# A streaming encoder step: three engines' queues in written order, units of 2048, softmax in ten pieces

## The chip, the cores and the metric

The kernel runs on one core of one Trainium2 chip. The metric is the device time of one execution in microseconds; the time before is 1638.82 us, the median of three runs (1638.69, 1638.82, 1639.95).

## The reference, cut to what matters

One layer of an encoder, for a prompt of 256 frames and a sample of 64 frames, which share the weights; D_MODEL is 2048, there are 8 heads of 128, 8 gating groups of 128, and 5632 is the width of the FFN. All is float32.

```
xn = rmsnorm(x)
q, k, v, u, vs, g = split(xn @ w_in)           # 5 x 1024 columns and 2 x 2048 gates
z = q k^T / sqrt(128); mask = k_pos < q_pos    # stick-breaking attention
log_stay = where(mask, log_sigmoid(-z), 0)
log_rest = cumsum(log_stay, reverse) - log_stay
a = where(mask, exp(log_sigmoid(z) + log_rest), 0) @ v
u, vs = gelu(u), rmsnorm(gelu(vs))
bb = u * (masked w_spatial @ vs + b_spatial)
g_a, g_b = sigmoid(g + b_gate)
merged = g_a * (a @ w_branch_a) + g_b * (bb @ w_branch_b)
h = x + merged @ w_out
h = h + (silu(hn @ w_gate) * (hn @ w_up)) @ w_down     # hn = rmsnorm(h)
y = rmsnorm(h)
```

New k, v and vs rows are outputs too. The sample's attention also sees 256 cached rows of k and v.

## The kernel before, in words

All 320 frames are the columns of every product; the 2048 features lie in 16 blocks of 128 partitions. Weights come from memory as blocks of 128 x 128, eight in a DMA of 512 KB issued on SP's queue, and each block is used once. A value is split into a high and a low part, and a product takes three matmuls for a weight block: high by high, high by low, low by high (`product`, L92 to L97). Two forms of the split are used:

- *Plain* (`weights`, `block`, L81 to L111): ACT casts the weights to fp32r (L87), DVE subtracts (L88). It serves the first six head blocks (`WHOLE`), all of `w_out`, and the first three pairs of the FFN (`PLAIN`).
- *Scaled fp16* (`Group`, L276): four tiles of 1024 columns share one scale. DVE takes a tile's largest value (L173) or ACT the sum of its absolutes (L178), DVE packs them (`pack`, L184, L186), one matmul spreads them over the partitions (`spread`, L190, into a bank of the products' own pool), DVE makes a power of two (`close`, L194). Then ACT writes the high half (L325) and DVE the low half (L326) right ahead of the matmuls that use them. It serves all the rest.

Features get their norm by `Features.normed` (L271): DVE multiplies by the factor of the column (L273), then `half` (L136) takes ACT's high half (L138) and DVE's low half (L139). A norm's root is taken on POOL (L219), copied on ACT (L224) and transposed on DVE (L226).

A *step* is eight weight blocks, thus 24 matmuls; `tick()` ends it, and `at(step, fn)` puts off work to the end of a step. I count steps from the end of the start stage, which makes q, k and v of heads 0 and 1 as x and the weights come in. Steps 0 to 11 are the six plain head blocks; 12 to 43 the other heads, with the spatial gate's `vs` and `us` behind them; then gates and the products by `w_a` and `w_b`; the plain products by `w_out` (32 steps); then the FFN, whose first 12 steps are plain. The attention goes by pairs of heads (`attend`, L713): `att_scores` (L587) takes the scores and the whole softmax (Abs, Exp and Ln on ACT at L617 to L619, scans on DVE, Exp), `att_turn` transposes the weights in 16-bit planes by a DMA on SP's queue, `att_join` (L546) puts them together on DVE, `att_out` (L664) multiplies by v, all between the steps of the heads that follow. One preload (L613) brings a table that holds both Exp and Ln.

The start stage is ordered by hand. Behind it a scheduler orders each engine's queue, but for instructions marked `keep_in_program_order`; SBUF holds ten raw tiles of 1024 and six split ones.

Of the kernel before, what the change touches and what calls it, by code (L numbers as in the profile page):

```python
# [33 lines left out]
AHEAD = 3  # L34
WHOLE = 6
BACK = 4
SLOTS = 49
RAW = 10
SPLIT = 6
LAG = 2  # L40
# [6 lines left out]
def stream_step(ctx: ExitStack, tc: tile.TileContext, xT, w_in, w_a, w_b, w_out, w_gu, w_down,  # L47
# [16 lines left out]
    def aux1():  # L64
        return psum.tile([P, 512], F32, tag="aux1", bufs=1, name="aux1")
# [5 lines left out]
    def at(tick, fn, *a):  # L71
        assert tick > state["tick"], (tick, state["tick"])
        later.setdefault(tick, []).append((fn, a))

    def tick():
        state["tick"] += 1
        for fn, a in later.pop(state["tick"], ()):
            fn(*a)


    def weights(src, n, view=lambda t: t):  # L81
        raw = wraw.tile([P, HALF * P], F32, tag="raw", bufs=RAW, name="raw")
        d = nc.sync.dma_start(out=view(raw[:, : n * P]), in_=src)
        if state["tick"] < 4:
            tc.keep_in_program_order(d)
        wh, wl = (wsplit.tile([P, HALF * P], F32R, tag="w", bufs=SPLIT, name=t) for t in ("wh", "wl"))
        nc.scalar.copy(out=wh[:, : n * P], in_=raw[:, : n * P])  # L87
        nc.vector.tensor_tensor(out=wl[:, : n * P], in0=raw[:, : n * P],  # L88
                                in1=wh[:, : n * P].bitcast(F32), op=ALU.subtract)
        return wh, wl  # L90
# [8 lines left out]
    def block(src, act, on=None):  # L99

        ps = acc()
        nk = len(act)
        if on is not None:
            nc.scalar.copy(out=ps[:, :T], in_=on)
        for k0 in range(0, nk, HALF):
            n = min(HALF, nk - k0)
            w = weights(src[:, k0 * P : (k0 + n) * P], n)
            for j in range(n):
                product(ps, w, j, act[k0 + j], on is None and k0 + j == 0, k0 + j == nk - 1)
            tick()  # L110
        return ps[:, :T]  # L111
# [54 lines left out]
    class Scale:  # L166

        def __init__(self, n, room):
            self.n, self.room = n, room
            self.tops = const.tile([P, n], F32, tag=f"tops{n}", bufs=2, name="tops")  # L170

        def top(self, i, src):
            tc.keep_in_program_order(nc.vector.tensor_reduce(  # L173
                out=self.tops[:, i : i + 1], in_=src, axis=mybir.AxisListType.X, op=ALU.max, apply_absolute_value=True))

        def sum(self, i, src, junk):
            tc.keep_in_program_order(
                nc.scalar.activation(out=junk, in_=src, func=AF.Abs, accum_out=self.tops[:, i : i + 1]))  # L178
# [9 lines left out]
        def spread(self):  # L188
            self.row = acc()
            tc.keep_in_program_order(nc.tensor.matmul(self.row[:, :P], self.own.to_broadcast([P, P]), turner, start=True, stop=True))  # L190
# [63 lines left out]
    class Features:  # L254
# [16 lines left out]
        def normed(self, m, src, factor):  # L271
            t = t320("ev")
            nc.vector.tensor_tensor(out=t, in0=src, in1=got[factor], op=ALU.mult)  # L273
            self.half.append(half(t, self.gain[:, m : m + 1]))

    class Group:  # L276

        def __init__(self, tiles, start, undo, by_vector, lead=(9, 7), first=0, home=None, late_undo=False):
            self.tiles, self.undo_of, self.by_vector, self.raw, self.home = tiles, undo, by_vector, [], home or wraw_tile
            n, now = len(tiles), state["tick"]  # L280
            for i in range(n):
                begin = max(start - lead[0] + i, first + i, now + 1)
                check = max(start - lead[1] + i, begin + 2)
                at(begin, self.load, i)
                at(check, self.top, i)
            ready = max(start + n - lead[1], check + 1)
            assert ready < start, (start, ready)
            at(ready, lambda: self.scale.spread())
            at(ready + 1, lambda: self.scale.close())
            at(max(ready + 1, start if late_undo else 0), self.settle)  # L290

        def load(self, i):
            src, n = self.tiles[i]
            raw = self.home()
            nc.sync.dma_start(out=raw[:, 0 : n * P], in_=src)
            self.raw.append(raw[:, 0 : n * P])

        def top(self, i):
            if i == 0:
                self.scale = Scale(len(self.tiles), W_ROOM)  # L300
            if i in self.by_vector:
                self.scale.top(i, self.raw[i])
            else:
                self.scale.sum(i, self.raw[i], junk[:, 0 : self.raw[i].shape[1]])
            if i == len(self.tiles) - 1:
                self.scale.pack()
# [9 lines left out]
        def block(self, i, n, x, on=None):  # L316
            ps, k = acc(), 0
            if on is not None:
                nc.scalar.activation(out=ps[:, :T], in_=on[0], func=AF.Copy, scale=on[1])
            nk = sum(c for _, c in self.tiles[i : i + n])  # L320
            for raw in self.raw[i : i + n]:
                w, up = raw.shape[1], self.scale.up
                both = wsplit.tile([P, 2, HALF * P], F16, tag="w", bufs=SPLIT, name="w16")
                wh, wl = both[:, 0], both[:, 1]
                nc.scalar.activation(out=wh[:, :w], in_=raw, func=AF.Copy, scale=up)  # L325
                nc.vector.scalar_tensor_tensor(out=wl[:, :w], in0=raw, scalar=up, in1=wh[:, :w],  # L326
                                               op0=ALU.mult, op1=ALU.subtract)
                for j in range(w // P):
                    product(ps, (wh, wl), j, x[k], on is None and k == 0, k == nk - 1)
                    k += 1  # L330
                tick()
            return ps[:, :T]

    class Acts:
# [4 lines left out]
        def add(self, r):  # L339
            self.scale.top(len(self.raw), r)  # L340
            self.raw.append(r)
            if len(self.raw) == self.n:
                now = state["tick"]
                at(now + 1, self.scale.pack)
                at(now + 2, self.scale.spread)
                at(now + 3, self.close)
                for k in range(self.n):
                    at(now + 3 + k // 3, self.split, k)
# [11 lines left out]
    def wraw_tile():  # L360
        return wraw.tile([P, HALF * P], F32, tag="raw", bufs=RAW, name="raw16")

    def tiles_of(w, k0=0, n=KD):
        return [(w[:, (k0 + k) * P : (k0 + min(k + HALF, n)) * P], min(HALF, n - k)) for k in range(0, n, HALF)]

    junk = const.tile([P, HALF * P], BF16, name="junk")
# [21 lines left out]
    def load_w(b, c, n):  # L388
        raw = wraw.tile([P, HALF * P], F32, tag="raw", bufs=RAW, name="raw0")
# [4 lines left out]
    def split_w(raw, n, chunks=None):  # L394

        if chunks and chunks.start:
            w = ws[-1]
        else:
            state["start"] = state.get("start", 0) + 1
            w = tuple(spool.tile([P, HALF * P], F32R, tag=t, name=t) if state["start"] % 4 == 0 else  # L400
                      wsplit.tile([P, HALF * P], F32R, tag="w", bufs=SPLIT, name=t) for t in ("wh", "wl"))
# [84 lines left out]

    attn = {}
    att_ctx = ExitStack()
    apool = att_ctx.enter_context(tc.tile_pool(name="attn", bufs=1))
    rooms = {}  # L490

    def gate_load():
        nc.gpsimd.memset(wso, 0.0)
        tc.keep_in_program_order(nc.sync.dma_start(out=wst.rearrange("p g t -> p (g t)"), in_=ws_t))
# [43 lines left out]
    def turn(src):  # L538
        to = planes("turned", src.shape[2])
        flat = lambda t: t.rearrange("p w n -> p (w n)")  # L540
        tc.keep_in_program_order(nc.sync.dma_start(
# [13 lines left out]
    def att_rows(p):  # L555
        cvt = attn[p]["cv"] = rooms["late"].tile([P, 2, 2, P], F32, tag="cv", name="cv")
        tc.keep_in_program_order(nc.sync.dma_start(out=cvt.rearrange("p i h d -> p i (h d)"),
# [29 lines left out]
    def att_scores(p):  # L587
        s = attn[p]
        q, k, qp = s["q"], s["k"], s["qp"]
        za, zs = (aux(), aux()), (aux(), aux())  # L590
# [4 lines left out]
        for j in range(2):  # L595
            for b in range(2):
                nc.tensor.matmul(zs[j][:, 0 : KT - TP], s["qs"][:, j].rearrange("p w t -> p (w t)"), s["ks"][j][b],
                                 start=b == 0, stop=b == 1)
        z = s["z"] = pair("z0"), pair("z1")[:, 0 : Z + TS]
# [491 lines left out]
```

## Time and profile before

| | |
|---|---|
| median of 3 runs | 1638.82 us |
| profiled execution, device time | 1640.53 us |
| its span | 1638.7 us |
| mean granted clock of the matmul engine | 0.991 |
| PE busy | 1600.8 us, 98% |
| DVE busy | 1135.5 us, 69% |
| ACT busy | 1012.3 us, 62% |
| POOL busy | 59.2 us, 4% |
| read from memory | 256.03 MB, 160 GB/s over the span |

The numbers are of one profiled execution, and the span is the time from its first to its last instruction. PE is the matmul engine, PEld its weight loads, DVE the vector engine, ACT the scalar engine, POOL the general one, SP the queue that issues most DMAs. Busy shares are means over stages with different limits; what a change in a stage is worth is read in that stage.

### The profile page before, as it was taken

The numbers are of one execution on the slowest core, as the hardware profiler recorded it, in microseconds if no ns is written. First come the engines' busy times: TensorE is split into PE (matmuls) and PEld (weight loads), VectorE is DVE, ScalarE is ACT, GpSimd is POOL, SyncE is SP. The second block draws the span as 40 slices with busy tenths as digits, with TensorE's granted clock in tenths as the row PEclk, the third lists the DMA queues.
The fourth block names the chain that finished last, engine by engine and source line by source line (L and its number), as shares of the span: only waits on it lengthen the run. The fifth ranks groups of instructions, "written<-read, shape, count | busy, mean of one in ns | idle before, by whom it ended". The sixth has DMA issues, their size and how long they took to land.

```text
span 1638.7 us, 28858 instructions
## 1 busy us (share of the span) xinstructions
PE 1600.8 (98%) x11662; PEld 1224.7 (75%) x11662; DVE 1135.5 (69%) x2013; ACT 1012.3 (62%) x1503; POOL 59.2 (4%) x80
## 2 busy tenths in 40 slices
PE   9979989999999999999999999999999999999997
PEld 9966657777777777999877777777777777777775
DVE  6978778986666674557866667666666776666785
ACT  6676776776566663445866666456666755665662
POOL 0111002000000000111000000000000000000000
PEclk9989989999999999999999999999999999999998
DMA  9557654654544554557554555445555454444421
GB/s 326 174 146 215 166 154 141 191 177 159 165 154 155 156 173 150 176 174 253 182 165 164 163 167 165 154 155 156 164 166 161 139 192 155 155 151 140 124 64 65
DMA packets 100518, 268.40 MB, mean 164 GB/s; under 512 B 28992, under 2 KB 35392, under 8 KB 100384
## 3 DMA queue, kind: packets, MB, share of 16 engines
q1 hardware_dynamic: 97936, 261.36, 50.7%
q0 software_dynamic: 1312, 3.80, 0.7%
q8 instruction: 91, 1.49, 0.4%
q10 hardware_dynamic: 1136, 1.39, 0.2%
q14 instruction: 43, 0.35, 0.1%
HBM read 256.03 MB, written 5.51 MB: 160 GB/s over the span
## 4 chain that ended last, share of the span: by engine, by line
PE 86%; DVE 6%; ACT 3%; DMA 3%; issue 1%; POOL 0%; SPq 0%; DVEq 0%; ACTq 0%; POOLq 0%
PE acc L97 28%; PE acc L95 28%; PE acc L96 28%; PE aux L415 1%; DMA raw<-w_in 1%; DMA turned<-wp 1%; PE acc L415 1%; DVE half L139 1%; DVE w L326 1%; DVE e L627 1%; DVE wl L88 1%; DVE tops L173 1%; DVE ev L273 0%; ACT wp L536 0%; DMA raw<-w_gu 0%
## 5 line engine op out<-in xcount | busy, mean ns | idle before, releaser
L97 PE MATMUL acc<-half,w 128*128 128x320 f16 x3232 | 968.4, 300 | 6.7 <-DVE w L326 6.6
L95 PE MATMUL acc<-half,w 128*128 128x320 f16 x3232 | 968.3, 300 | 1.1 <-DVE q L690 0.5
L96 PE MATMUL acc<-half,w 128*128 128x320 f16 x3232 | 968.2, 300 | 0.0
L326 DVE SCALAR_TENSOR_TENSOR w<-raw,up,w 128x1024 f16<-128x1024 f32 (+1 forms) x412 | 517.8, 1262 | 142.6 <-ACT w L325 133.2
L325 ACT ACTIVATE w<-raw,up 128x1024 f16<-128x1024 f32 (+1 forms) x412 | 454.6, 1122 | 198.7 <-DVE up L196 179.9
L97 PEld LDWEIGHTS <-w 128*128 128x128 f16 x3232 | 316.4, 98 | 140.7 <-DVE w L326 9.1
L95 PEld LDWEIGHTS <-w 128*128 128x128 f16 x3232 | 316.5, 98 | 123.8 <-ACT w L325 0.7
L96 PEld LDWEIGHTS <-w 128*128 128x128 f16 x3232 | 316.4, 98 | 120.2 <-issue 1.2
L178 ACT ACTIVATE junk<-raw 128x1024 bf16<-128x1024 f32 x263 | 274.7, 1044 | 33.1 <-DMA raw<-w_b 19.3
L173 DVE TENSOR_REDUCE tops<-raw 128x1 f32<-128x1024 f32 (+1 forms) x149 | 171.9, 1154 | 12.2 <-DMA raw<-w_in 12.2
L194 DVE TENSOR_REDUCE peak<-acc 128x1 f32<-128x128 f32 x118 | 33.8, 286 | 166.1 <-PE acc L190 165.9
L941 ACT ACTIVATE bb<-acc,undo 128x320 f32<-128x320 f32 x41 | 21.6, 527 | 148.2 <-PE acc L97 144.3
L87 ACT CAST wh<-raw 128x1024 fp32r<-128x1024 f32 x56 | 58.6, 1046 | 73.2 <-PE acc L96 61.9
L88 DVE TENSOR_TENSOR wl<-raw,wh 128x1024 fp32r<-128x1024 f32 x56 | 68.4, 1222 | 31.5 <-ACT wh L87 27.8
L95 PE MATMUL acc<-mh,wh 128*128 128x320 f32 x256 | 79.3, 310 | 0.0
L96 PE MATMUL acc<-ml,wh 128*128 128x320 f32 x256 | 79.2, 309 | 0.0
L97 PE MATMUL acc<-mh,wl 128*128 128x320 f32 x256 | 79.2, 309 | 0.0
L965 DVE SCALAR_TENSOR_TENSOR h<-acc,undo,h 128x320 f32<-128x320 f32 x47 | 25.8, 548 | 57.0 <-PE acc L97 53.5
L178 ACT ACTIVATION_READ_ACCUMULATOR junk<-raw 128x1 f32 x263 | 49.3, 187 | 0.0
L95 PEld LDWEIGHTS acc<-mh,wh 128*128 128x128 f32 x256 | 48.1, 188 | 0.0
L96 PEld LDWEIGHTS acc<-ml,wh 128*128 128x128 f32 x256 | 48.1, 188 | 0.0
L97 PEld LDWEIGHTS acc<-mh,wl 128*128 128x128 f32 x256 | 48.1, 188 | 0.0
(224 smaller groups left out, 1205.5 us busy)
## 6 DMA issues: line engine op xcount, KB each, us to landing
raw<-w_gu SPq DMA_DIRECT2D x176, 512.0 KB, 4.5
raw<-w_in SPq DMA_DIRECT2D x141, 512.0 KB, 4.6
raw<-w_down SPq DMA_DIRECT2D x80, 512.0 KB, 4.2
raw<-w_out SPq DMA_DIRECT2D x32, 512.0 KB, 3.7
raw<-w_a SPq DMA_DIRECT2D x16, 512.0 KB, 3.6
raw<-w_b SPq DMA_DIRECT2D x16, 512.0 KB, 4.1
raw<-w_down SPq DMA_DIRECT2D x16, 256.0 KB, 3.4
x<-xT SPq DMA_DIRECT2D x8, 320.0 KB, 7.7
```

Of the source, the lines that this page charges most:

```text
L87: nc.scalar.copy(out=wh[:, : n * P], in_=raw[:, : n * P])
L88: nc.vector.tensor_tensor(out=wl[:, : n * P], in0=raw[:, : n * P], in1=wh[:, : n * P].bitcast(F32), op=ALU.subtract)
L95: nc.tensor.matmul(ps[:, :T], a, x[0], start=first, stop=False, skip_group_check=True)
L96: nc.tensor.matmul(ps[:, :T], a, x[1], start=False, stop=False, skip_group_check=True)
L97: nc.tensor.matmul(ps[:, :T], b, x[0], start=False, stop=last, skip_group_check=True)
L173: tc.keep_in_program_order(nc.vector.tensor_reduce(out=self.tops[:, i : i + 1], in_=src, axis=mybir.AxisListType.X, op=ALU.max, apply_abso ...
L178: nc.scalar.activation(out=junk, in_=src, func=AF.Abs, accum_out=self.tops[:, i : i + 1]))
L194: nc.vector.tensor_reduce(out=top, in_=self.row[:, :P], axis=mybir.AxisListType.X, op=ALU.max)
L325: nc.scalar.activation(out=wh[:, :w], in_=raw, func=AF.Copy, scale=up)
L326: nc.vector.scalar_tensor_tensor(out=wl[:, :w], in0=raw, scalar=up, in1=wh[:, :w], op0=ALU.mult, op1=ALU.subtract)
L415: nc.tensor.matmul(first[b][h][:, :T], w[:, (h * n + j) * P : (h * n + j + 1) * P], xs[c + j][i], start=not last and c + j + i == 0, stop= ...
L965: nc.vector.scalar_tensor_tensor(out=hs[i], in0=ps, scalar=g.undo, in1=hs[i], op0=ALU.mult, op1=ALU.add)
```

## The change

- Behind the start stage the queues of SP, ACT, DVE and PE are in the order in which the code issues (`manual_schedule`); only POOL's is left to the scheduler. Work that is due at the end of a step is sorted by a rank.
- `Plain` replaces `weights` and `block`: the load is issued eight steps ahead, the high half two steps ahead, the low half one.
- `Group` now has one unit of 2048 columns for each two steps (two units in the FFN), with a scale for each group: loads 10 (FFN: 14) steps ahead, bound 3 later, high half three steps ahead, low half two. There are 148 spreads instead of 118, and they have a bank of their own (`aux1`). SBUF holds five raw and three split units of 2048.
- Epilogues of products come one step later.
- `normed` multiplies in place (the x of the first norm) or into one buffer (`mg`, the FFN's).
- The softmax of a pair is in ten pieces from step +3 to +11 of the pair; its outputs come at +18. Pairs 0 to 3 begin at steps 10, 21, 33 and 45. The preload of the table of Exp and Ln is gone; the built program has 24 table loads (6 before).
- Four gate blocks are between the plain heads and the others (`EARLY_GATES`), evicted by a Copy, with their Sigmoid later; the gates lead the merge by 5 blocks (2 before).
- At the end the last block's residual is put into PSUM some steps ahead.

```diff
-    def at(tick, fn, *a):
+    def at(tick, fn, *a, rank=5):
+        if tick <= state["tick"]:
+            fn(*a)
+        else:
+            later.setdefault(tick, []).append((rank, fn, a))
     def tick():
         state["tick"] += 1
-        for fn, a in later.pop(state["tick"], ()):
+        for _, fn, a in sorted(later.pop(state["tick"], ()), key=lambda x: x[0]):
             fn(*a)
...
+    class Plain:
+        def __init__(self, src, nk, start):
+            self.src, self.nk, self.start, self.w = src, nk, start, {}
+            for j, k0 in enumerate(range(0, nk, HALF)):
+                at(start + j - 8, self.load, j, rank=0)
+                at(start + j - 2, self.high, j, rank=1)
+                at(start + j - 1, self.low, j, rank=1)
...
-        def normed(self, m, src, factor):
-            t = t320("ev")
+        def normed(self, m, src, factor, home=None):
+            t = src if home is None else home
             nc.vector.tensor_tensor(out=t, in0=src, in1=got[factor], op=ALU.mult)
             self.half.append(half(t, self.gain[:, m : m + 1]))
...
+        def __init__(self, units, start, undo, lead, by_vector=(), late_undo=False):
...
+                at(s - lead + 3, self.bound, u, u in by_vector, rank=4)
+                at(s - 3, self.high, u, rank=2)
+                at(s - 2, self.low, u, rank=2)
+            last = start + 2 * len(units) - 2 - lead
+            at(last + 4, lambda: self.scale.pack(), rank=3)
+            at(last + 5, lambda: self.scale.spread(), rank=1)
+            at(last + 6, self.close, late_undo, rank=1)
...
+    ctx.enter_context(tc.manual_schedule(engines=ENGINES))
...
+    def att_soft(p, i):
+        s = attn[p]
+        zz = s["z"][i]
+        e = pair("e")[:, : zz.shape[1]]
+        nc.scalar.activation(out=e, in_=zz, func=AF.Abs)
+        nc.scalar.activation(out=e, in_=e, func=AF.Exp, scale=-1.0)
+        nc.scalar.activation(out=e, in_=e, func=AF.Ln, bias=1.0)
+        s.setdefault("e", {})[i] = e
...
     def attend(p, now):
...
+        at(now + 3, att_scores, p, 0)
+        at(now + 4, att_gather, p, 0)
+        at(now + 4, att_scores, p, 1)
+        at(now + 5, att_gather, p, 1)
+        at(now + 5, att_turn, p, "vt")
+        at(now + 6, att_soft, p, 1)
+        at(now + 7, att_softened, p, 1)
+        at(now + 7, att_soft, p, 0)
+        at(now + 8, att_scan, p, 1)
+        at(now + 8, att_softened, p, 0)
+        at(now + 9, att_scan, p, 0)
+        at(now + 9, att_join, p, "vt")
+        at(now + 10, att_exp, p, 0)
+        at(now + 11, att_exp, p, 1)
+        at(now + 13, att_turn, p, "wt")
+        at(now + 16, att_join, p, "wt")
+        at(now + 18, att_out, p)
...
     for m in range(KD):
-        at(base + 3 + m // 2, lambda m=m: ffn.normed(m, hs[m], "rh"))
+        at(base + 3 + m // 2, lambda m=m: ffn.normed(m, hs[m], "rh", t320("mg", 1)))
```

Three places show what moves on the engines. The first is DVE's queue in the plain heads at the start (`ev`, `x` and `half` are the features on their way to halves, `wl` or `w` 128x1024 the low half of a plain weight), before and after:

```order
L694 SCALAR_TENSOR_TENSOR q<-acc,rx 128x320
L273 TENSOR_TENSOR ev<-x,rx 128x320 x2
L88 TENSOR_TENSOR wl<-raw,wh 128x1024
L139 SCALAR_TENSOR_TENSOR half<-ev,gain_629,half 128x320 x2
L273 TENSOR_TENSOR ev<-x,rx 128x320 x2
L88 TENSOR_TENSOR wl<-raw,wh 128x1024
L139 SCALAR_TENSOR_TENSOR half<-ev,gain_629,half 128x320 x2
```
```order
L743 TENSOR_TENSOR k<-acc,rx 128x320
L195 TENSOR_REDUCE tops<-raw 128x1
L294 TENSOR_TENSOR x<-x,rx 128x320
L161 SCALAR_TENSOR_TENSOR half<-x,gain_608,half 128x320
L294 TENSOR_TENSOR x<-x,rx 128x320
L161 SCALAR_TENSOR_TENSOR half<-x,gain_608,half 128x320
L123 TENSOR_TENSOR w<-raw,w 128x1024
L215 TENSOR_REDUCE peak<-row 128x1
L216 TENSOR_TENSOR down<-peak,bits 128x1
L217 TENSOR_TENSOR up<-down,bits 128x1
L342 TENSOR_SCALAR undo<-down,undo_610 128x1
L352 SCALAR_TENSOR_TENSOR w<-raw,up,w 128x2048
```

Multiplies and halves stood in pairs, and now they alternate; a bound of 2048 columns and a 2048-wide low half stand among them. The second is ACT's queue in the softmax of the first pair (`e` and `z` are its scores):

```order
L613 ACT_TABLE_LOAD
L617 ACTIVATE e<-z_1020 128x640
L138 ACTIVATE half<-ev,gain_629 128x320
L618 ACTIVATE e<-e 128x640
L617 ACTIVATE e<-z_1021 128x448
L619 ACTIVATE e<-e 128x640
L618 ACTIVATE e<-e 128x448
L138 ACTIVATE half<-ev,gain_629 128x320
L619 ACTIVATE e<-e 128x448
```
```order
L655 ACTIVATE e<-e 128x448
L656 ACT_TABLE_LOAD
L656 ACTIVATE e<-e 128x448
L349 ACTIVATE w<-raw,up 128x2048
L822 ACTIVATE gate<-acc,undo 128x320
L199 ACTIVATE junk,tops<-raw 128x2048
L654 ACTIVATE e<-z_1263 128x640
L655 ACT_TABLE_LOAD
L655 ACTIVATE e<-e 128x640
L656 ACT_TABLE_LOAD
L656 ACTIVATE e<-e 128x640
```

The two halves of the pair now have the wide work of the weights between them, and tables are loaded between Exp and Ln. The third is DVE's queue at the start of the FFN (`h` is the residual, `rh` the factor of its norm):

```order
L88 TENSOR_TENSOR wl<-raw,wh 128x1024
L226 STREAM_TRANSPOSE rh<-root 128x320
L273 TENSOR_TENSOR ev<-h,rh 128x320 x2
L139 SCALAR_TENSOR_TENSOR half<-ev,gain_7846,half 128x320 x2
L273 TENSOR_TENSOR ev<-h,rh 128x320 x2
L88 TENSOR_TENSOR wl<-raw,wh 128x1024
L139 SCALAR_TENSOR_TENSOR half<-ev,gain_7846,half 128x320 x2
```
```order
L123 TENSOR_TENSOR w<-raw,w 128x1024
L195 TENSOR_REDUCE tops<-raw 128x1
L294 TENSOR_TENSOR mg<-h,rh 128x320
L161 SCALAR_TENSOR_TENSOR half<-mg,gain_7755,half 128x320
L294 TENSOR_TENSOR mg<-h,rh 128x320
L161 SCALAR_TENSOR_TENSOR half<-mg,gain_7755,half 128x320
L123 TENSOR_TENSOR w<-raw,w 128x1024
L205 TENSOR_REDUCE topmost<-tops 128x1
L207 TENSOR_SCALAR packed<-topmost 128x1
L294 TENSOR_TENSOR mg<-h,rh 128x320
L161 SCALAR_TENSOR_TENSOR half<-mg,gain_7755,half 128x320
```

Here too the pairs are gone: each multiply stands behind the half before it.

More of the change, by code (lines that the diff above doesn't have):

```diff
@@ L34 @@
 AHEAD = 3
+BACK = 4
 WHOLE = 6
[L36 to L40, printed above, removed]
+EARLY_GATES, LAG = 4, 5
+SLOTS = 51
+RAW = 5
+SPLIT = 3
+UNIT = 2 * HALF * P
 W_ROOM = 2.0 ** -13
@@ L188, in spread @@
         def spread(self):
-            self.row = acc()
-            tc.keep_in_program_order(nc.tensor.matmul(self.row[:, :P], self.own.to_broadcast([P, P]), turner, start=True, stop=True))
+            self.row = aux1()
+            nc.tensor.matmul(self.row[:, :P], self.own.to_broadcast([P, P]), turner, start=True, stop=True)
         def close(self):
@@ L276, in stream_step @@
     class Group:
[L278 to L290, printed above, removed]
@@ new lines, in load, with bound @@
+        def load(self, u, src, k, n):
+            if k == 0:
+                self.raw[u] = raw_unit()
+            nc.sync.dma_start(out=self.raw[u][:, k * P : (k + n) * P], in_=src)
+        def bound(self, u, by_vector):
+            if u == 0:
+                self.scale = Scale(len(self.units), W_ROOM)
+            src = self.raw[u][:, : self.width[u]]
+            if by_vector:
+                self.scale.top(u, src)
+            else:
+                self.scale.sum(u, src, junk[:, : self.width[u]])
@@ L308, in settle, with close @@
+        def close(self, late_undo):
+            self.scale.close()
+            if not late_undo:
+                self.settle()
         def settle(self):
@@ L314, in settle, with high, low, block @@
             self.undo = self.undos[0]
[L316 to L331, printed above, removed]
+        def high(self, u):
+            w = split_unit().bitcast(F16).rearrange("p (h k) -> p h k", h=2)[:, :, : self.width[u]]
+            self.w[u] = w[:, 0], w[:, 1]
+            nc.scalar.activation(out=w[:, 0], in_=self.raw[u][:, : self.width[u]], func=AF.Copy, scale=self.scale.up)
+        def low(self, u):
+            nc.vector.scalar_tensor_tensor(out=self.w[u][1], in0=self.raw.pop(u)[:, : self.width[u]], scalar=self.scale.up,
+                                           in1=self.w[u][0], op0=ALU.mult, op1=ALU.subtract)
+        def block(self, u, x, first=0, n=None, into=None):
+            n = n or self.width[u] // P
+            assert state["tick"] == self.start + 2 * u + (first > 0), (state["tick"], self.start, u)
+            ps = into or acc()
+            for k in range(n):
+                product(ps, self.w[u], first + k, x[k], into is None and k == 0, k == n - 1)
+                if k % HALF == HALF - 1 or k == n - 1:
+                    tick()
             return ps[:, :T]
@@ L358, in split @@
             self.half.append(half(self.raw[k], self.up))
[L360 to L366, printed above, removed]
+    last = const.tile([P, T], F32, name="last")
+    junk = const.tile([P, UNIT], mybir.dt.uint8, name="junk")
     w_qkv = w_in[0 : 3 * H].rearrange("(b h) p k -> b p h k", h=H)
@@ new lines, in stream_step, with block16, gate_block, gate_open @@
+    out_start = start
+    outs = [Plain(w_out[m], KD, out_start + 2 * m) for m in range(KD)]
+    ffn_start = out_start + 2 * KD
+    def block16(n, x):
+        g = groups.pop(("in", n))
+        return g.block(0, x), g.undo
+    gate = {}
+    def gate_block(m, i):
+        ps, undo = block16(5 * H + i * KD + m, mixed.half)
+        gt = gate[m, i] = slot(dt=F32, name="gate")
+        at(state["tick"] + 1, lambda: nc.scalar.activation(out=gt, in_=ps, func=AF.Copy, scale=undo), rank=2)
+    def gate_open(m):
+        for i in range(2):
+            nc.scalar.activation(out=gate[m, i], in_=gate[m, i], func=AF.Sigmoid, bias=b_gate[:, i * KD + m : i * KD + m + 1])
@@ L925, in stream_step, with residual @@
             now += 2
+    at(out_start + 4, ffn.measure)
+    at(out_start + 6, ffn.scale.spread)
+    at(out_start + 8, ffn.close)
+    (hs, ypair), hg = halves(KD, "h"), []
+    sq = Squares("sq_h")
+    def residual(m, ps, x):
+        nc.vector.tensor_tensor(out=hs[m], in0=ps, in1=x, op=ALU.add)
+        hg.append(gained(hs[m], g_ffn[:, m : m + 1]))
+        sq.add(hs[m], nc.vector if m == KD - 1 else None)
+    for m in range(KD):
+        x = t320("ev")
+        nc.sync.dma_start(out=x, in_=xT[:, m, :])
+        ps = outs[m].block(merged)
+        if m < KD - 1:
+            at(state["tick"] + 1, residual, m, ps, x, rank=2)
+        else:
+            residual(m, ps, x)
@@ new lines, in stream_step, with gated @@
+    mctx.close()
+    nh = norm("rh", sq.total, D)
+    at(state["tick"] + 2, lambda: got.update(rh=nh.spread()))
+    sqf = Squares("sq_f")
+    PIECES = (slice(0, P), slice(P, T))
+    keep = tc.keep_in_program_order
+    rooms["raw"] = pool("late")
+    base = state["tick"]
+    assert base == ffn_start
+    for m in range(KD):
+        at(base + 3 + m // 2, lambda m=m: ffn.normed(m, hs[m], "rh", t320("mg", 1)))
+    def gated(s, pg, pu, g):
+        t, u = t320("ev"), t320("bb")
+        if g is None:
+            nc.vector.tensor_tensor(out=t, in0=pg, in1=got["rh"], op=ALU.mult)
+            nc.scalar.activation(out=t, in_=t, func=AF.Silu)
+            nc.vector.tensor_tensor(out=u, in0=pu, in1=got["rh"], op=ALU.mult)
+        else:
+            nc.scalar.activation(out=t, in_=pg, func=AF.Silu, scale=g.undo)
+            nc.scalar.activation(out=u, in_=pu, func=AF.Copy, scale=g.undo)
+        r = slot(dt=F32, name="act")
+        nc.vector.tensor_tensor(out=r, in0=u, in1=t, op=ALU.mult)
+        acts[s].add(r)
@@ L946, in stream_step @@
+        end = s == 2 and i == KD - 1
+        g, u = groups.pop((kind, s, i))
+        if not end:
+            ps = g.block(u, acts[s].half)
+            if s == 2 and i == KD - 2:
+                downed(s, i, ps, g)
+            else:
+                at(state["tick"] + 1, downed, s, i, ps, g, rank=2)
         if s == 2 and i == 0:
```

451 lines of the change are left out of this document (221 added, 230 removed).

## The prediction

> **What bounds the kernel now.** I read the page's busy shares first, then the stretches in which the matmul engine stands still, then the waits there, and last the single instructions of the engines that it waits for.
>
> The busy line of the page, and the busy times of consecutive stretches (start and end, length, then busy us and instruction count of PE, PEld, DVE, ACT, POOL, then the granted clock, the DMA share and GB/s):
>
> ```profile
> PE 1600.8 (98%) x11662; PEld 1224.7 (75%) x11662; DVE 1135.5 (69%) x2013; ACT 1012.3 (62%) x1503; POOL 59.2 (4%) x80
> ...
> 48.20:105.80 57.60, 47.94 (x309) 46.88 (x308) 52.27 (x97) 43.03 (x78) 8.03 (x11) 0.91 0.46 143
> ...
> 106.00:330.00 224.00, 207.41 (x1519) 151.01 (x1518) 181.18 (x340) 156.21 (x265) 26.88 (x34) 0.98 0.63 174
> 330.00:760.00 430.00, 430.00 (x3126) 342.72 (x3124) 274.69 (x481) 238.84 (x330) 15.20 (x14) 1.00 0.51 163
> 760.00:800.00 40.00, 38.44 (x262) 38.07 (x261) 35.72 (x68) 30.24 (x52) 1.98 (x1) 1.00 0.68 244
> 800.00:1600.00 800.00, 800.00 (x5930) 577.22 (x5929) 537.29 (x930) 503.42 (x716) 0.00 (x0) 1.00 0.48 154
> ```
>
> PE is busy throughout 330 to 760 and 800 to 1600 us: nothing that ACT, DVE or the DMAs do there can shorten the run. It stands still for 9.7 us in the first stretch, 16.6 in the second (the attention) and 1.6 at 760 to 800 (where the FFN begins). Only there, and at the end, can this change win; and wherever it makes PE wait, it loses. Next the waits of PE (engine, what it writes, line; the engine and line waited for; us in total, times, longest), and stretches round the long ones:
>
> ```profile
> PE acc L190 <- ACT vs L780: 8.2, 1, 8.2
> PE acc L97 <- DVE w L326: 6.6, 6, 2.0
> PE acc L190 <- DVE packed L186: 6.2, 3, 4.4
> PE aux L592 <- DVE q L694: 5.2, 1, 5.2
> ```
> ```profile
> 96.00:100.00 4.00, 3.62 (x14) 3.62 (x15) 2.25 (x9) 4.00 (x9) 0.00 (x0) 0.50 0.66 191
> 120.00:124.00 4.00, 2.02 (x15) 1.26 (x14) 4.00 (x8) 3.69 (x5) 0.00 (x0) 1.00 0.08 22
> 228.00:232.00 4.00, 0.09 (x2) 0.08 (x2) 0.00 (x0) 3.98 (x6) 0.00 (x0) 0.50 0.23 41
> 232.00:236.00 4.00, 4.00 (x17) 2.21 (x17) 3.71 (x8) 3.71 (x7) 1.57 (x2) 0.50 0.00 0
> 236.00:240.00 4.00, 4.00 (x24) 2.59 (x23) 3.15 (x5) 3.71 (x7) 0.89 (x1) 0.76 0.48 134
> 1040.00:1240.00 200.00, 200.00 (x1483) 144.21 (x1482) 125.07 (x202) 121.41 (x168) 0.00 (x0) 1.00 0.50 160
> ```
>
> The last row gives the price of a step: 200/1483 = 0.1349 us for a matmul, 3.24 for the 24 of a step. After the 8.2 us wait the clock stands at 0.50: 17 and 24 matmuls where 4 us hold 29.6, so (12.6 + 5.6) x 0.1349 = 2.5 us more. After 2 us without work (120 to 124) it stays at 1.00.
>
> **The change, part by part.** All durations are from the profiled run, 1640.5 us of device time (span 1638.7), 1.7 above the median of 1638.8.
>
> *Start, steps 0 to 11.* Their matmuls are f32r; one of 24 goes by this row:
>
> ```profile
> 37.66 3.58 PE acc L415 x24
> ```
>
> I take 3.52 for a clean step, 42.2 for twelve, and 1.2 for the score matmuls in between: before loses 57.6 - 42.2 - 1.2 = 14.2. What DVE must do in this time, with the hand-over of one feature block:
>
> ```profile
> L88 DVE TENSOR_TENSOR wl<-raw,wh 128x1024 fp32r<-128x1024 f32 x56 | 68.4, 1222 | 31.5 <-ACT wh L87 27.8 <-PE acc L97 3.6
> L139 DVE SCALAR_TENSOR_TENSOR half<-ev,gain,half 128x320 f16<-128x320 f32 x32 | 17.5, 565 | 0.2 <-ACT half L138 0.2
> L273 DVE TENSOR_TENSOR ev<-x,rx 128x320 f32<-128x320 f32 x16 | 7.4, 484 | 0.1
> ```
> ```profile
> 59.52 0.48 DVE L273 TENSOR_TENSOR ev<-x,rx 128x320 f32<-128x320 f32 x1
> ...
> 60.05 0.56 ACT L138 ACTIVATE half<-ev,gain 128x320 f16<-128x320 f32 x1 [0.76 <-DVE ev L273]
> ...
> 60.87 0.55 DVE L139 SCALAR_TENSOR_TENSOR half<-ev,gain,half 128x320 f16<-128x320 f32 x1
> ```
>
> The new order has multiply, half, multiply, half on DVE, and the half needs ACT's part of the same block. So DVE stands through ACT's 0.56 each time: 0.484 + 0.05 + 0.556 + 0.03 + 0.565 = 1.69 for a block, where multiplies and halves in pairs take 1.05. Two blocks and one low half of a weight are 2 x 1.69 + 1.22 = 4.60 of DVE for each of the eight steps 2 to 9, against 3.52 of PE. The chain begins at 56.4 (before 52.4), since the copies of the root stand behind ACT's next cast, which waits for the end of step 0 at 51.7. 56.4 + 36.8 is 93.2; four head epilogues of 0.48 and a 2048-wide maximum of 2.3, less small overlaps, bring it to 96.1. In step 10 a 2.36 us low half stands ahead of the pack (100.2), and the spread of step 11 waits for that: fp16 products begin at 103.8, where 90.4 would be free of loss. 13.4 lost for 14.2: **-0.7**. The cover is thin; a half clock behind the 6 us gap would make it +2.
>
> *Attention and spatial gate, steps 12 to 92.* Before loses the 16.6 and 2.5 at half clock, 19.1. What ACT has there (the first and last of 24 groups of attention rows, L536 to L679, which sum to 61.4 for four pairs, 15.3 a pair):
>
> ```profile
> L536 ACT COPY wp<-z 128x1280 uint16<-128x1280 uint16 x4 | 5.0, 1257 | 0.1
> ...
> L679 ACT COPY aT<-aux 128x64 f32<-128x64 f32 x4 | 0.9, 218 | 0.0
> ```
> ```profile
> L325 ACT ACTIVATE w<-raw,up 128x1024 f16<-128x1024 f32 x396 | 444.4, 1139 | 197.7 <-DVE up L196 179.9 <-PE acc L97 11.0 <-DVE undo L312 5.8
> L325 ACT ACTIVATE w<-raw,up 128x512 f16<-128x512 f32 x16 | 11.3, 709 | 1.0 <-PE acc L97 1.0
> L326 DVE SCALAR_TENSOR_TENSOR w<-raw,up,w 128x1024 f16<-128x1024 f32 x396 | 506.2, 1283 | 142.6 <-ACT w L325 133.2 <-DMA raw<-w_gu 8.7
> L178 ACT ACTIVATE junk<-raw 128x1024 bf16<-128x1024 f32 x263 | 274.7, 1044 | 33.1 <-DMA raw<-w_b 19.3 <-DMA raw<-w_in 7.5 <-DMA raw<-w_a 6.0
> ```
> ```profile
> 229.64 0.40 ACT L536 COPY wp<-wown 128x256 uint16<-128x256 uint16 x1
> 230.04 1.28 ACT L780 ACT_TABLE_LOAD   x1
> 231.34 0.94 ACT L780 ACTIVATE vs<-acc,undo 128x320 f32<-128x320 f32 x2
> ```
>
> The kernel now loads activation tables 24 times instead of 6, since Exp and Ln no longer share one; a load starts where the copy before it ends and the next instruction follows its end by 0.02, so I price 18 more at 1.28 each, 23 us of ACT. ACT's load is then (156 + 23)/205 = 87% of the time that PE needs for the stretch, DVE's 181/205 = 88%, both in a fixed order; before, whatever was ready went first. I laid the two queues out step by step. Twelve steps cost PE 12 x 3.24 + 4.6 of attention matmuls = 43.5. ACT has six 2048-wide high halves of 2.0 (1.139 and two times 0.430 more, by the 512- and 1024-wide rows), four bounds of 2.09, four epilogues of 0.52, 15.3 of attention and four loads: 42.8, less 1.8 of overlap. To that come its waits: its cast of the turned weights stands behind DVE's join, which waits for the transpose of the exponentials in step 26,
>
> ```profile
> 142.50 7.95 DMA turned<-wp
> ```
>
> 6.0 us by my layout, and 3.7 behind the join of v in step 30. 41.0 + 9.7 is 50.7 for 43.5; with the slack that the buffers carry, steps 24 to 35 lose 6.8. In the same way steps 12 to 23 lose 1.1, 36 to 47 5.1, 48 to 59 (loads for Gelu and the squares join in) 11.3, and the rest to 92 about 3: 27.3 in all, **+8.2**. From below, the stretch could lose nothing (-19); from above, if each of three pairs lost 11.3, 38 (+19). I stay with the layout, whose waits have rows.
>
> The Trainium skill ("ScalarE: Activation LUTs", What ACT_TABLE_LOAD costs) adds a drain of 1.38 us to each switch, 2.66 together; the row above shows 1.28 and no gap. By it 18 switches would be 48 us of ACT instead of 23, and the sum about 25 higher.
>
> *Spreads.* Each unit of two steps has its own scale: 148 spreads instead of 118.
>
> ```profile
> 411.60 0.22 PE L190 MATMUL acc<-turner,packed 128*128 128x128 bf16 x1
> 411.66 0.30 PE L95 MATMUL acc<-half,w 128*128 128x320 f16 x1
> ```
>
> The next product starts 0.06 later: 30 x 0.06 = **+1.8**.
>
> *Start of the FFN, steps 196 to 207.* Here before has the multiplies and halves in pairs:
>
> ```profile
> 768.20 0.90 DVE L273 TENSOR_TENSOR ev<-h,rh 128x320 f32<-128x320 f32 x2
> 769.32 1.02 DVE L139 SCALAR_TENSOR_TENSOR half<-ev,gain,half 128x320 f16<-128x320 f32 x2 [0.23 <-ACT half L138]
> ```
>
> Now there is one buffer, and each multiply follows the half before it. With the first product of step 196 as zero, the factor is there at 9.5; steps 199 to 206 cost DVE 4.60 each, 36.8, and 4.2 go to two gated products (three of 0.49 each), packs and closings: 50.5. The low half for step 207 follows at 51.6, its products take 3.5, and step 208 starts at 55.1 instead of 42.3. 12.8 lost, 1.6 before: **+11.2**. Below, with ACT's part hidden, it is 1.6 again (0); above, with 3.5 more of waits in this order and a half clock, +17.
>
> *At nothing:* the wide halves and sums (ACT saves 0.28 a unit, DVE 0.2) and the gate epilogues lie beside 200 of 200 us of PE, with DVE 125 and ACT 121 busy; without that cover ACT's gain is 0.28 in 6.5. Loads run 8 to 14 steps ahead, 26 us or more against the landing of some 5, so a transpose that waits on SP's queue ahead of them delays none that is due, unless it waits over 20 us. The end prepares its last block earlier, at most 0.5 of the last idle time.
>
> Sum: -0.7 + 8.2 + 1.8 + 11.2 = +20.5: 1661.0 as profiled, 1659 as median.
>
> **The rivals.** *Worse: half clock after each stop.* The layout has some six stops of 3.5 to 6.4 us; the 4.4 before 96 and the 8.2 before 232 were both followed by 0.50, 2 us at 120 was not. Four stops at 2.5 are 10 more, 1669 (1664 to 1676). The Trainium skill ("TensorE: Matmul & The Clock Gate", Part 1) puts the limit at an idle window of 3.4 us; the two rows agree, and no row has a stop between 2 and 4 us.
>
> *The FFN's chain is hidden.* If steps 196 to 207 run as before, because the layout has the order of ACT's halves too late, 11 fall away: 1648. Against it speaks that DVE has 35.72 of 40 already there.
>
> *Faster: fixed order ends the attention's stops.* The 8.2 us stop of a spread behind ACT's vs comes from a whole softmax that sits ahead of it on ACT; ten pieces with 2048-wide work between them may let that be. If the attention loses under 3.5 in all, less than 1 a pair, the term is -16, and with +9 to the rest 1632. It decides below 10 lost in the attention when the FFN is hidden too. Against it: 88% load on two engines that wait for each other.
>
> *Each table load drains.* If ACT also empties round each load, about one short activation is lost with it (0.71, the 512-wide row): 16 x 0.71 = 11 in steps 12 to 59, mostly on the path, 1670. The gap of 0.02 behind the one load shown speaks against it; the Trainium skill's rule above is this case, at about twice the price.
>
> **How the numbers follow.** The sum as it stands 0.43 (own range 1648 to 1672, of the attention's +-8 and the FFN's +-4), half clock 0.20, FFN hidden 0.18, faster 0.12, drained loads 0.03, and 0.04 for terms that cancel to within 0.2% (3.3 us, about what a measurement of this kernel can tell from no change). The range leaves out the faster side and the drained loads: 1640 to 1676. Faster 0.12, same 0.04, slower 0.84.
>
> **What would show it.** In the new profile: PE idle at the first 50 to 105 us about as before, ended by the pack; waits of PE for DVE's low halves (L123) round 770 to 810 of over 8 us in sum; ACT with 24 table loads, and waits of PE for ACT's high halves or DVE's low halves spread over all four pairs; 100% PE behind the first fp16 step of the FFN. I am wrong if DVE's multiplies at the FFN's start show no gaps in front of the halves, or if the attention's PE idle is under 10 us.

## The result, and the profile after

The changed kernel takes 1680.39 us (median of 4; 1678.69 to 1682.18) against 1638.76 in the same runs: 1.0253 times as long, interval 1.0236 to 1.0271. It is 41.6 us slower where I had forecast 20; the time lies 4 us above my range. The profiled execution has a span of 1680.4 at a clock of 0.985.

The changed kernel's busy line, then stretches of it (columns as in the prediction; they begin with the first matmul of step 0, of step 12, of the FFN, and of the FFN's fp16 part; `w_out`, between the second and the third, is left out):

```profile
PE 1615.0 (96%) x11692; PEld 1235.4 (74%) x11692; DVE 1095.5 (65%) x1819; ACT 1009.1 (60%) x1119; POOL 57.3 (3%) x80
...
48.36:108.17 59.81, 47.78 (x294) 46.12 (x292) 43.81 (x78) 32.72 (x49) 7.43 (x10) 0.89 0.46 147
108.17:654.29 546.12, 527.47 (x3901) 382.85 (x3900) 379.80 (x745) 393.60 (x464) 26.01 (x34) 0.99 0.53 163
767.15:838.60 71.45, 49.57 (x293) 48.42 (x291) 41.00 (x73) 32.21 (x44) 4.03 (x1) 0.88 0.41 138
838.60:1680.40 841.80, 829.79 (x6136) 598.51 (x6134) 533.68 (x798) 473.90 (x452) 2.10 (x3) 0.99 0.43 151
```

The same stretches of the kernel before:

```profile
48.12:105.77 57.65, 47.99 (x310) 46.93 (x308) 52.24 (x97) 43.01 (x78) 8.11 (x11) 0.91 0.46 143
105.77:644.24 538.47, 521.88 (x3856) 378.27 (x3854) 389.41 (x745) 348.02 (x530) 26.89 (x34) 0.99 0.56 167
757.11:801.44 44.33, 42.77 (x292) 42.30 (x291) 38.38 (x72) 33.55 (x56) 1.98 (x1) 1.00 0.68 241
801.44:1638.70 837.26, 827.97 (x6136) 597.55 (x6135) 557.80 (x977) 512.42 (x733) 2.09 (x3) 1.00 0.47 150
```

By length: the start +2.2, the attention and the gates +7.7, `w_out` between them 0, the FFN's twelve plain steps +27.1, the rest +4.5. The FFN's plain steps are the loss: PE is busy for 49.57 of 71.45, at a clock of 0.88. What PE waits for now (of the whole execution), and what SP's queue waits for at 760 to 845:

```profile
PE row L211 <- DVE packed L207: 40.2, 16, 7.0
PE acc L100 <- DVE w L123: 13.9, 5, 8.0
```
```profile
SPq L322 <- DVE w L123: 51.9, 5, 15.4
SPq L115 <- DVE w L123: 17.4, 2, 12.2
SPq L322 <- DVE w L352: 13.1, 2, 12.1
```

Over the whole execution most stops are a spread (L211) that waits for its pack (L207); of the 21.9 us of idle time in the FFN's plain steps, 12.5 are two products that wait for DVE's low half of the plain weights (L123), and 9.4 two spreads. And the loads of weights (L322, L115), which I had at nothing, stand for up to 15 us until DVE's low half frees a raw unit. Before, loads waited for the same reason at this place (750 to 808), but for 7.9 at most:

```profile
SPq L295 <- DVE wl L88: 24.9, 7, 7.9
SPq L83 <- DVE wl L88: 12.0, 4, 4.8
```

What that does is seen on ACT and then on DVE, some 35 us into the FFN:

```profile
801.03 1.91 ACT L199 ACTIVATE junk<-raw 128x2048 uint8<-128x2048 f32 x1 [5.83 <-DMA raw<-w_gu]
802.85 0.18 ACT L199 ACTIVATION_READ_ACCUMULATOR junk<-raw 128x1 f32 x1
802.94 0.55 ACT L160 ACTIVATE half<-mg,gain 128x320 f16<-128x320 f32 x1
```
```profile
796.17 0.48 DVE L294 TENSOR_TENSOR mg<-h,rh 128x320 f32<-128x320 f32 x1
803.52 0.55 DVE L161 SCALAR_TENSOR_TENSOR half<-mg,gain,half 128x320 f16<-128x320 f32 x1 [6.87 <-ACT half L160]
```

A bound on ACT (L199) waits 5.83 for its weights; the next feature's half (L160) stands behind it in written order, and DVE's low half (L161) behind that, 6.87. Behind that stands, on DVE, the low half of the plain weights (L123, at 805.69), for which PE waits 7.98 here, and which frees the raw unit for the next loads: they go out at 806.98. In all, bounds wait for their weights like this (767 to 842):

```profile
ACT junk L199 <- DMA raw<-w_gu: 8.5, 2, 5.8
DVE tops L195 <- DMA raw<-w_gu: 3.2, 1, 3.2
```

### The profile page after: what moved, and what is told of

Its sections match the earlier page's. It is cut to its first block, busy times and chain, and to the rows that moved or that the text cites. A ratio compares the mean times of both kernels' runs of the same rounds, so it can differ in the third digit from the quotient of the medians.

```text
span 1680.4 us, 28045 instructions
## 1 busy us (share of the span) xinstructions
PE 1615.0 (96%) x11692; PEld 1235.4 (74%) x11692; DVE 1095.5 (65%) x1819; ACT 1009.1 (60%) x1119; POOL 57.3 (3%) x80
## 4 chain that ended last, share of the span: by engine, by line
PE 83%; DVE 7%; ACT 7%; DMA 2%; issue 2%; SPq 0%; ACTq 0%; DVEq 0%
PE acc L98 26%; PE acc L99 26%; PE acc L100 26%; DVE w L352 2%; PE aux L444 2%; ACT junk L199 1%; ACT w L349 1%; DMA raw<-w_gu 1%; DVE w L123 1%; PE acc L444 1%; ACT half L160 1%; PE row L211 1%; DMA raw<-w_in 1%; DVE tops L195 0%; DVE half L161 0%
## 5 line engine op out<-in xcount | busy, mean ns | idle before, releaser
L349 ACT ACTIVATE w<-raw,up 128x2048 f16<-128x2048 f32 (+1 forms) x206 | 405.6, 1969 | 413.6 <-PE acc L100 398.2
L352 DVE SCALAR_TENSOR_TENSOR w<-raw,up,w 128x2048 f16<-128x2048 f32 (+1 forms) x206 | 475.2, 2307 | 55.6 <-ACT w L349 55.0
L199 ACT ACTIVATE junk<-raw 128x2048 uint8<-128x2048 f32 (+1 forms) x149 | 277.8, 1865 | 8.5 <-DMA raw<-w_gu 8.5
L195 DVE TENSOR_REDUCE tops<-raw 128x1 f32<-128x2048 f32 (+1 forms) x57 | 127.7, 2241 | 3.2 <-DMA raw<-w_gu 3.2
L215 DVE TENSOR_REDUCE peak<-row 128x1 f32<-128x128 f32 x148 | 42.3, 286 | 133.7 <-PE row L211 133.6
L120 ACT CAST w<-raw 128x1024 fp32r<-128x1024 f32 x56 | 58.7, 1047 | 82.4 <-PE acc L100 70.1
L123 DVE TENSOR_TENSOR w<-raw,w 128x1024 fp32r<-128x1024 f32 x56 | 77.7, 1390 | 14.1 <-ACT w L120 14.1
L98 PE MATMUL acc<-mh,w 128*128 128x320 f32 x256 | 79.3, 310 | 0.0
L99 PE MATMUL acc<-ml,w 128*128 128x320 f32 x256 | 79.1, 309 | 0.0
L100 PE MATMUL acc<-mh,w 128*128 128x320 f32 x256 | 79.1, 309 | 0.0
L211 PE MATMUL row<-turner,packed 128*128 128x128 bf16 x148 | 32.8, 222 | 41.4 <-DVE packed L207 40.2
L100 PE MATMUL acc<-S,w 128*128 128x320 f32 x144 | 47.6, 331 | 13.2 <-DVE w L123 13.2
L211 PEld LDWEIGHTS <-packed 128*128 128x128 bf16 x148 | 14.5, 98 | 50.6 <-DVE packed L207 45.4
L98 PEld LDWEIGHTS acc<-mh,w 128*128 128x128 f32 x256 | 48.1, 188 | 0.0
L99 PEld LDWEIGHTS acc<-ml,w 128*128 128x128 f32 x256 | 48.1, 188 | 0.0
```

The source lines that it names most:

```text
L98: nc.tensor.matmul(ps[:, :T], a, x[0], start=first, stop=False, skip_group_check=True)
L99: nc.tensor.matmul(ps[:, :T], a, x[1], start=False, stop=False, skip_group_check=True)
L100: nc.tensor.matmul(ps[:, :T], b, x[0], start=False, stop=last, skip_group_check=True)
L120: nc.scalar.copy(out=self.w[j][0], in_=self.raw[:, j * HALF * P : (j + 1) * HALF * P])
L123: nc.vector.tensor_tensor(out=self.w[j][1], in0=self.raw[:, j * HALF * P : (j + 1) * HALF * P], in1=self.w[j][0].bitcast(F32), op=ALU.subt ...
L195: nc.vector.tensor_reduce(out=self.tops[:, i : i + 1], in_=src, axis=mybir.AxisListType.X, op=ALU.max, apply_absolute_value=True)
```

## The experiments

All start from the changed kernel. The times are medians; "FFN steps" is the length of the twelve plain steps (42.2 would be free of loss), "attention" that from step 12 to `w_out`, both of the profiled execution. That execution can lie off the median (the changed kernel's 1.8 above it, e3_both's 2.4 below), so differences of stages and of medians need not agree to the last microsecond.

| kernel | us | start | attention | FFN steps |
|---|---|---|---|---|
| before | 1638.8 | 57.7 | 538.5 | 44.3 |
| changed | 1680.4 | 59.8 | 546.1 | 71.4 |
| e1_pairs | 1671.2 | 59.4 | 546.0 | 64.1 |
| e2_late | 1667.3 | 58.8 | 544.5 | 59.1 |
| e12_lead | 1669.9 | 58.8 | 545.3 | 59.1 |
| e3_both | 1662.9 | 58.6 | 544.5 | 52.3 |
| e4_table | 1667.8 | 59.5 | 532.1 | 71.6 |
| e6_all | 1641.7 | 50.5 | 532.3 | 52.3 |
| e8_sched | 1640.9 | 51.2 | 532.3 | 48.8 |
| e7_act | 1633.2 | 51.1 | 532.3 | 49.3 |
| e11_pack | 1629.9 | 47.6 | 530.6 | 49.6 |
| e9_spread | 1656.3 | 44.7 | 564.1 | 47.8 |
| e10_only | 1701.3 | 53.9 | 576.4 | 70.8 |

**Pairs in the FFN.**

```diff
-        at(base + 3 + m // 2, lambda m=m: ffn.normed(m, hs[m], "rh", t320("mg", 1)))
+        at(base + 3 + m // 2, lambda m=m: ffn.two(m, hs[m : m + 2], "rh", [t320("mg", 1), t320("ev")]))
```

> At the start of the FFN two multiplies stand ahead of two halves on DVE (two buffers), nothing else differs from the changed kernel. Theory A (loads): the 12 plain steps lose 29 us, of which my chain of multiplies and halves is only 13; the rest comes from bounds on ACT and DVE that wait for weights which SP could not ask for, since its next load waits in line for a free raw unit. Then pairs save 16 x 0.6 = 10 us of DVE's chain at most, and the bounds still wait: 4 to 8 us less, 1672 to 1676. Theory B (alternation): the alternate order is the whole loss, and the loads are late only because DVE frees the raw units late: the chain is 10 shorter and the half clock of up to 7 us goes with it, 14 to 20 less, 1660 to 1666.

9.2 less, 7.4 of it in the FFN steps: just over what A gave, far from B. The bounds wait for their weights as before (8.6 on ACT, 3.5 on DVE). The alternation is a part of the loss, not the whole.

**Late bounds.**

```diff
-                at(s - lead + 3, self.bound, u, u in by_vector, rank=4)
+                at(s - lead + wait, self.bound, u, u in by_vector, rank=4)     # wait=6 in the FFN, pack to close with it
```

> In the FFN's groups bound, pack, spread and close come three steps later, the loads where they were. A: the waits of the bounds for their weights (5.8 and 2.6 on ACT, 3.2 on DVE) go, and some half clock: 10 to 14 less, 1666 to 1670. B: the work of DVE is the same and its order hardly differs: 0 to 3 less, 1677 to 1681.

13.1 less, 12.3 in the FFN steps, with the loads asked where they were and the work the same: A. No bound there waits for its weights any more. Bound, pack, spread and close moved together, so what each of them is worth alone is not shown. The w_down groups, for which three steps were too late, got four new stops of 0.5 and 1.4.

**Both.**

> Pairs and late bounds together. A: both terms go, and with them the half clock: 22 to 27 less than the changed kernel, 1653 to 1658, with PE's idle time in the first 12 FFN steps under 4 us. B: no more than pairs alone.

17.5 less, short of A's 22. In the FFN steps the two add up (19.1 of 7.4 + 12.3), but 6.4 of PE's idle time stay where A gave under 4.

**Loads 11 steps ahead**, with the bounds where the late bounds stood:

```diff
-... now, lambda: [ffn.undo], 14, (1,) if made % 2 else ())
+... now, lambda: [ffn.undo], 11, (1,) if made % 2 else ())     # and the same for w_down's groups
```

> The changed kernel with the FFN's groups loaded 11 steps ahead instead of 14; bound, pack, spread and close move with them, so the bounds stand where the late bounds stood. If SP's asking too early is what makes the loads late (a load that waits for a free raw unit holds up the plain loads behind it): as good as late bounds or better, 1662 to 1667. If the loads need their 14 steps, or the bounds still come before their weights: 1672 or more.

The median, 1669.9, lies between the two forecasts. But the FFN steps are as long as with late bounds to 0.1, though all was asked three steps later, and in both runs loads go out 8.2, 16.9, 28.4, 39.7 and 53.3 us into the FFN. (What is longer lies outside these steps: 0.8 in the attention, which the edit does not touch, and 1.7 behind them, with the same 13.3 of idle time.) So in these steps early asking neither helps nor harms: a load goes out when a raw unit comes free, and the place of the bound counts.

**The table.**

```diff
+        if i == 1:
+            nc.scalar.preload_act_table_set("natural_log_exp_and_others")
```

> Only the softmax's table differs: one that holds both Exp and Ln is asked for ahead of each pair's first Exp, 11 table loads instead of 24. If ACT's load in the attention sets the steps there, as my sum had it: 13 x 1.28 = 17 us of ACT less, of which 3 to 8 us reach the end, 1672 to 1677. If the waits of the spreads there come from DVE's queue alone: 0 to 1, 1679 to 1681.

12.6 less, 14.0 in the attention. The trace has 12 loads, not 11, and 9 instead of 21 in this stretch: 14.0 is most of the 15.4 us that 12 loads take. More than I expected: ACT there had little slack. PE's idle time in the stretch falls from 18.7 to 8.4; the other 3.7 come from its busy time, for the same 3901 matmuls, with the mean clock at 1.00 instead of 0.99:

```profile
107.56:639.70 532.14, 523.76 (x3901) 382.07 (x3900) 379.08 (x745) 377.97 (x452) 26.46 (x34) 1.00 0.55 167
```

It is now 6.3 shorter than before the change.

**All of them, and pairs at the start.** `mixed.two` in place of two `mixed.normed`, in place.

> Late bounds and pairs in the FFN, the table of Exp and Ln, and now also pairs of multiplies and halves in the start stage's features (in place, no new buffer). If the alternation makes the start's loss, as my sum had it, DVE needs 2 x 1.05 + 1.22 = 3.3 for a step where it needed 4.6, under PE's 3.5: the twelve plain steps fall from 59 to 49 to 52, and the kernel to 1637 to 1642. If another wait of that stage (the pack behind a 2048-wide low half, the casts on ACT) takes over: 57 to 59, and 1646 to 1649.

The start falls from 58.6 to 50.5, in the middle of what the first theory gave; the whole is where I put it, 1.0018 times the kernel before (1.0009 to 1.0028).

**The first FFN bounds on ACT**, late ones for these groups alone:

```diff
-... now, lambda: [ffn.undo], 14, (1,) if made % 2 else ())
+... now, lambda: [ffn.undo], 14, (1,) if made % 2 and made > 8 else (), wait=6 if made <= 8 else 3)     # made: place in the FFN's order
```

> As the kernel with all four edits, but the late bounds only for the first FFN groups, whose bounds all go to ACT. If what is left at the FFN's start (52 for 42 us of PE) is DVE's work, two maxima of 2.3 leave it: 46 to 49 for the twelve steps; and the two later stops of 1.9 us each, which late bounds brought to the w_down groups, go. 8 to 11 less than with all four. If the features' halves now wait for ACT instead: 52 or more, and 4 less.

8.4 less, as the first theory gave: 3.0 in the FFN steps (49.3, just over its 46 to 49), and 4.6 behind them, where the four late stops are gone. 0.9971 of the kernel before (0.9960 to 0.9982).

**The scheduler in the FFN's plain steps.**

```diff
+    hand.close()          # manual_schedule ends at the first FFN step ...
...
+        if n_order == PLAIN:
+            by_hand()     # ... and begins again behind the plain pairs
```

> Table, pairs at the start, and no edit in the FFN but one: its first 12 steps are left to the scheduler, with the single buffer and the early bounds of the changed kernel. If the written order of the queues is what loses there, it comes back to 44 to 48 us. If the single buffer and the number of raw units lose it whatever the order: 55 to 70.

48.8, just over the first forecast, but the fp16 steps behind are 8.2 longer than in e7_act: 3.9 us are stops in which halves are late (L160 and L161 by turns), and PE is busy for 3.8 longer with as many matmuls. Over the whole FFN it is 18.5 less than the changed kernel, so the order costs some 18 of its 31.6 us. What the other 13 come from (the single buffer, the number of raw units, the early bounds) this run does not show.

**Spreads one step later**, in the best kernel so far and in the changed kernel alone:

```diff
-            at(last + 5, lambda: self.scale.spread(), rank=1)
-            at(last + 6, self.close, late_undo, rank=1)
+            at(last + 6, lambda: self.scale.spread(), rank=1)
+            at(last + 7, self.close, late_undo, rank=1)
```

> The kernel with the four edits and its first FFN bounds on ACT, and every spread and close one step later (the late bounds two steps later, not three). If the stops that are left, all but a few of a spread behind its pack, are a matter of place (the pack stands behind a 2048-wide low half, and the spread one step on): the stop of 5.8 at the start falls by 3.2 and its half clock goes, the attention's 8.6 fall under 3, 1621 to 1627. If DVE and ACT are behind there by their work: the stops come back at the halves, 1631 to 1634.

> The changed kernel with nothing but its spreads and closes one step later. 40 of its 56 us of PE's waits are spreads behind packs, 16 times. By place: the stops in the attention (18.6 us, none over 2.9) nearly all go, with their half clock 15 to 20, and some of the FFN's: 1658 to 1668. By the work of DVE and ACT (13 table loads too many among it): the same time is lost at the next wait, 1676 to 1680.

Both are misses: 23.1 and 20.9 slower. The start does gain (51.1 to 44.7, its stop gone, and 59.8 to 53.9), but the attention loses 32 and 30, and PE's waits of the second change their name:

```profile
PE row L211 <- DVE peak L215: 36.0, 15, 7.8
PE acc L100 <- DVE w L123: 26.0, 10, 5.9
```

The spread now waits for its bank, until DVE has read the row before (L215). The step that the spread gained was taken from between the close and the high half; the close stands behind the attention's round trips of DVE and ACT, and the high half needs it at once. So the fault is neither of my two: with one bank for the row, the chain pack, spread, close, high half has no step to spare there. Whether a second bank would let the spread pass was not tried.

**Pack ahead of the low half**, for groups of one unit whose bound is on DVE (the FFN's groups keep their order):

```diff
-            at(last + 4, lambda: self.scale.pack(), rank=3)
+            at(last + 4, lambda: self.scale.pack(), rank=1 if 0 in by_vector else 3)
```

> The kernel with the four edits and its first FFN bounds on ACT, and the pack of a group whose bound was on DVE now stands ahead of the epilogues and the 2048-wide low half of its step, not behind them. If my step for the start holds (the spread of step 11 waits for a pack behind a low half): the stop of 5.8 falls by the 2.9 of that low half and the half clock with it, and each third spread in the attention waits less; 3 to 6 less than the 1633.2, 1627 to 1630. If the pack only ends later for another reason: 0 to 1 less.

3.4 less by the medians; in the profiles the start is 3.5 shorter and the attention 1.7. The start's stop falls from 5.84 to 3.23, about the low half of 2.9 that stood ahead. At 0.9944 of the kernel before (0.9930 to 0.9957) it is the best version.

## Why the prediction was wrong, point by point

- *Start, -0.7; measured +2.2.* The mechanism stands: pairs there take 8.1 us away, and the pack ahead of the low half 3.5. PE's idle time (12.0) was near my 13.4; what I left out is 4.8 of work at half clock (PE busy for 47.78; for 42.97 in e9_spread, whose clock is 1.00 there), which I had named at +2 and not taken. The comparison was also uneven: of the 14.2 that I gave to before, only 9.7 was idle time, while my 13.4 was idle time alone. And the first pair's 18 score matmuls, which I priced at 1.2, have left this stretch for the attention, so on the prediction's own count the start loses 59.8 - 42.2 = 17.6 for 14.2, 3.4 more and not 2.2.
- *Attention, +8.2, and most of the spreads' +1.8; measured +7.7.* Near in the sum, in part by luck: the 45 more matmuls of this stretch are 28 spreads (1.7 by my price) and the first pair's scores (1.2), so 4.8 is left for the queues where I gave 8.2, and this offsets what the start had too little. I looked for PE's waits at high and low halves; they are all spreads behind packs. ACT's two waits of my layout, 6.0 behind the join of the weights and 3.7 behind that of v, are here as 5.0 and 3.4 at their longest, in ACT's waits at 110 to 350:

```profile
ACT S L593 <- DVE av L574: 10.3, 3, 3.4
ACT S L593 <- DVE wt L574: 5.2, 2, 5.0
```

  What I had not seen is how the sum is made up: the added table loads cost 14.0, and without them the stretch is 6.3 shorter than before, in spite of its 45 more matmuls. The rival in which the written order ends the attention's stops was right without the added tables, in direction: idle time falls from 16.6 to 8.4, not under its 3.5. (Its 1632 takes +9 for the rest, where the terms of the sum give 12.3; it should read 1635.)
- *A load at 1.28.* Right: 24 loads of 1283 ns, with 0.1 us of idle time in all before the eight at L656; the added drain has no support here, since 12 loads fewer gave back 14.0, less than their own 15.4.
- *FFN, +11.2; measured +27.1, and 4.5 behind it.* This is the step that failed. The alternation is as I priced it, one block in 1.69:

```profile
785.02 0.48 DVE L294 TENSOR_TENSOR mg<-h,rh 128x320 f32<-128x320 f32 x1
786.13 0.55 DVE L161 SCALAR_TENSOR_TENSOR half<-mg,gain,half 128x320 f16<-128x320 f32 x1 [0.63 <-ACT half L160]
786.71 0.49 DVE L294 TENSOR_TENSOR mg<-h,rh 128x320 f32<-128x320 f32 x1
```

  and pairs take back 7.4 of my 12.8. The term that failed is one that I put at nothing, "Loads run 8 to 14 steps ahead": a load is issued when a raw unit is free, whatever its place in the order, and the bounds in front of the features' halves wait for it (11.7 in all). That is worth 12.3 (late bounds). Of the 27.1, both edits together give back 19.1 and the bounds on ACT 3.0; 5.0 stay open. The 4.5 behind these steps is a last stop of 2.69, a spread behind its pack, with its half clock; it is gone with the four edits and the bounds on ACT.
- *Half clock.* I gave it 0.20 as a rival and left it out of the sum. In the FFN steps it is 6.4 (PE busy for 49.57; for 43.21 in e9_spread, whose clock is 1.00 there), in the start 4.8, in the attention about the 3.7 that went with the table loads. It came on top of the stops, as that rival said, but the stops of the FFN were longer and had another cause than the layout's.
- *100% PE behind the FFN's start:* right, after that last stop. *Wide halves, gates between heads, the end at nothing:* `w_out` and the fp16 FFN show no loss; the gates and the width were not tried alone.

What stays open is why e11_pack still takes 49.6 for the FFN's plain steps, 5 more than before; its stops there are 1.3, 0.5, 0.8 and 2.0.

## What to carry to other kernels

A load ahead of time is free only while a buffer is free: where one queue order is written for all engines, price each load by the instruction that frees its buffer, and put the first reader no earlier than that. In such an order an instruction that waits for a DMA or another engine stops all behind it; here work in pairs, and short work that others wait for ahead of long work, brought back some 19 of the 50 us between the changed kernel and the best one, for a second buffer in the FFN. A function that needs another table is a cost on an engine that is full, not a detail: 12 loads cost 14 us here.

## What the runs showed of the hardware that I had not expected

The clock halved after stops shorter than I had taken for safe. In the changed kernel two stops of the same length, 2.39 us, ended at 195.50 and 245.28; behind the first the granted clock was 0.58, behind the second it stayed full. Stops of 2.85, ended at 280.78, and of 2.76, at 298.90, lowered it too:

```profile
195.50:199.50 4.00, 4.00 (x18) 2.39 (x19) 3.93 (x9) 4.00 (x7) 0.56 (x1) 0.58 0.91 221
245.00:249.00 4.00, 3.72 (x28) 2.85 (x29) 3.93 (x11) 3.94 (x5) 0.00 (x0) 1.00 0.78 239
280.70:284.70 4.00, 3.92 (x18) 2.33 (x19) 3.49 (x7) 0.74 (x2) 0.00 (x0) 0.60 0.84 274
298.80:302.80 4.00, 3.90 (x19) 2.35 (x20) 2.90 (x6) 3.91 (x5) 1.92 (x2) 0.60 0.77 232
```

That is 18 or 19 matmuls in 4 us. So the length alone does not decide. The same holds from run to run: in the run of late bounds, which does not touch the attention, the stop at the same place of the program, 2.83 us long and ended at 277.59, was followed by a full clock:

```profile
277.50:281.50 4.00, 3.91 (x30) 2.85 (x31) 3.50 (x7) 0.72 (x2) 0.00 (x0) 1.00 0.81 265
```

30 matmuls for 18 after the same stop: 12 x 0.135 = 1.6 us, half the stop again, are lost or not. The Trainium skill ("TensorE: Matmul & The Clock Gate", Part 1) has the clock fall after an idle window of 3.4 us that runs freely; the runs here show it after less. A stop of 1.83 (e1_pairs, ended at 261.33) was followed by a clock of 0.73 over 4 us, and one of 3.39 (e2_late, ended at 799.42) by 1.00. Between these two lengths the length does not tell whether the price is paid; what does is not shown.
